# One hybrid encoder layer on one core: the triangular inverse moves from GpSimd and TensorE to VectorE, the weights' low parts from VectorE to GpSimd

## The chip, the core and the metric

The kernel runs on one core of one Trainium2 chip, from one launch. The metric is the device time of one execution in microseconds, lower is better. Engines are named as the profile names them: PE (TensorE matmul) and PEld (its weight loads), DVE (VectorE), ACT (ScalarE), POOL (GpSimd) and SP (SyncE, which here only issues DMAs).

## The reference

One layer for 512 tokens of a new stream and 8 running streams of 16 tokens each, 640 tokens in all, model width 1024, in fp32. Everything is a projection of the same normalised input:

```python
h = rmsnorm(x, norm_g)
proj = h @ w_in                     # 1024 -> 10368 columns
# A: stick-breaking attention, 16 heads of 64 (causal, 128 past keys for the running streams)
# B: RWKV-7 recurrence, 16 heads of 64, one state S (64x64) per head
S = S * w_t + (S @ -kk_t) (kk_t * a_t)^T + v_t k_t^T ;  o_t = S @ r_t
y_a = (o_a * silu(z_a)) @ w_o_a ;  y_b = (norm(o_b) * silu(z_b)) @ w_o_b
x = x + (sigmoid(g_a) * y_a + sigmoid(g_b) * y_b) @ w_out ;  y = rmsnorm(x, final_norm_g)
```

Outputs are y, the new keys and values, the last projected rows of B and the states S.

## The kernel before

**Jobs.** Each projection is cut into jobs of 128 output columns: 81 from `w_in`, 8 each from `w_o_b` and `w_o_a`; `w_out` follows in its own loop. fp32 products are made of three passes of a reduced fp32 type: the weight block `raw` (128 x 1024) is split into a high part `whi` (ACT, `wsplit`, line 486) and a low part `wlo` (DVE, `wlow`, line 494), the input into `xh` and `xl`. A job has two halves of 320 tokens, each 8 blocks of depth by 3 passes, so 48 matmuls (`gemm_range`, line 499). While job i runs, the weights of i+2 are loaded, and i+1 is split: `whi` after the second depth block, `wlo` after the fourth. `raw`, `whi` and `wlo` have two buffers each.

**Streams.** Beside the jobs run generators, called streams: for each of 8 pairs of RWKV heads `prep` (decays, keys, the matrices A of each chunk of 64 tokens), `prep2` (the inverse below), `samp`, `chain` (8 chunk steps one behind the other, each PE, ACT, PE, ACT, PE, DVE), `sstate` and `post`; later for each of 8 pairs of attention heads `aprep` and `attn`. `chain(p)` waits for `chain(p-1)`. A planner (`Clock`, `Driver.run`, line 303) keeps an estimated time for each engine and tile while the program is written out: at each `yield` it lets every stream whose inputs are ready by that estimate issue its next piece, by priority, and then goes on with the job. The result is one fixed order of instructions on each engine; on the chip every engine takes its own in that order, each waiting for its inputs. In the running job there is a `yield` after every second depth block (line 537). `calm()` (line 707) holds a stream back while DVE is planned more than 1.6 us ahead of PE.

**Order of the jobs.** The list `mixed` holds the RWKV projections R, K, V of each pair, `free` those of attention (q, k, v, z) and gates; a mixed job is taken when its condition `soon` holds, otherwise a free one (`job`, line 456). For V of pair p the condition is that `chain(p-3)` is done (line 1519). When `post` of the last pair is done, attention opens (`open_attn`, line 1569), beside the remaining jobs.

**The inverse (`prep2`, line 875).** For each pair and chunk the inverse of (I - A), A strictly lower triangular 64x64, is built. The four diagonal 32x32 blocks of all ten chunks are gathered in `STG` (ACT), transposed by 32x32 on DVE so that each partition holds one block in `INV`, and solved there by forward substitution: step j multiplies row j with column j below it and adds. Before the change this runs on 16x16 blocks, two at a time, on POOL: 14 steps of two instructions for each pair (lines 895 to 901). Then the 16x16 inverses are joined to 32x32 by two rounds of small matmuls (32 and 48 for each pair, lines 916 to 948, with the mask `half`), and after that, unchanged by the diff, to 64x64.

**State of the running streams (`sstate`, line 1094).** For each of two groups the rows X are spread over 4 streams by a mask (`ux`, POOL) and multiplied with the keys: two matmuls of 64 output rows and 256 columns for each group into one PSUM tile, and one addition on DVE.

**Opening (`start`, line 566).** Five token tiles are loaded, squared (ACT), scaled (DVE) and transposed (PE, `put`); `norm_g` is spread over the partitions by a DMA, all loads are issued by SP, and the first sums of squares become factors for tiles 0, 1 and 2, 3 and 4. `warm` are matmuls on zeros that keep PE running.

Of the kernel before, what the change touches and what calls it, by code (L numbers as in the profile page):

```python
# [340 lines left out]
def body(tc, ins, outs, dbg=None):  # L341
# [100 lines left out]
    half = cpool.tile([128, 2], F32, name="half")  # L442
# [51 lines left out]
    def wlow(i):  # L494
        if i < len(jobs):
            j = jobs[i]
            vtt(j.lo, j.raw, j.hi.bitcast(F32), ALU.subtract)

    def gemm_range(i0, i1):
# [6 lines left out]
        for i in range(i0, i1):  # L506
# [9 lines left out]
            for half in range(2):  # L516
# [5 lines left out]
                for k in range(8):  # L522
# [43 lines left out]
    def start():  # L566
        x34 = pers.tile([128, 2, D], F32, tag="H", name="x34")
        srow = pers.tile([88, 3, 128], F32, tag="V", name="srow", bufs=3)
        with pool("start", bufs=1) as sp:
            xt = [sp.tile([128, D], F32, tag="x", name="x", bufs=3) for _ in range(3)]  # L570
            xt += [x34[:, 0], x34[:, 1]]

            def loadx(i):
                dma(out=xt[i], in_=ins["x_prompt"][0, i * 128:(i + 1) * 128, :] if i < 4 else
                    ins["x_sample"].rearrange("b t d -> (b t) d"))
            gb = sp.tile([128, D], F32, name="gb")
            wz = sp.tile([128, 512], BF16, name="wz")
            V.memset(wz, 0.0)
            psw = bank("g")
# [5 lines left out]

            warm(18)
            loadx(0)
            dma(out=gb, in_=ins["norm_g"].partition_broadcast(128).rearrange("p o d -> p (o d)"))
            loadx(1)
            dma(out=ident, in_=ins["consts"][:, 0:128])  # L590
            loadx(2)
            wload(0)
            loadx(3)
            loadx(4)
# [10 lines left out]
            sv = sp.tile([128, 5], F32, name="sv")  # L605
            sr = sp.tile([128, 5], F32, name="sr")
            st = sp.tile([128, 5], F32, name="st")
            junk = sp.tile([128, D], F32, name="junk")
# [4 lines left out]
            def rstd(i0, i1):  # L613
                c = slice(i0, i1)
# [9 lines left out]
            def pscale(i):  # L624
                G.tensor_scalar(out=xt[i], in0=xt[i], scalar1=sr[:, i:i + 1], scalar2=1.0, op0=ALU.mult, op1=ALU.mult)
                gtt(xt[i], xt[i], gb, ALU.mult)

            square(0)
            rstd(0, 1)
            scale(0)  # L630
            square(1)
            square(2)
            rstd(1, 3)
            scale(1)
            put(0, xt[0], "ab")
            warm(6)
            wsplit(0)
            scale(2)
            put(1, xt[1], "ab")
            warm(3)  # L640
            wlow(0)
            square(3)
            square(4)
            put(2, xt[2], "ab")
            warm(0)
# [53 lines left out]
    def setf(*k):  # L699
        flags[k] = True  # L700
# [27 lines left out]
    def prep(p):  # L728
# [9 lines left out]
        if p + 1 < NPAIR:  # L738
            rwkv_load(p + 1)
# [1040 lines left out]
```

## Time and profile before

| what | value |
|---|---|
| three runs, us | 1167.69, 1173.54, 1175.17; median 1173.54 |
| the profiled execution, us | 1171.08 |
| its span from first to last instruction, us | 1169.3 |
| mean granted TensorE clock | 0.99 |

The span is what the profile divides; 1.8 us of the execution lie around it. Busy times are unions of an engine's instructions, those on PE with modelled ends, so a busy PE can still be late. All engines' work is recorded by a helper at line 213, so groups are told apart by tile names; a tile name without a number stands for all its buffers.

### The profile page before, as it was taken

What the parts mean: (1) busy time and instruction counts of PE and PEld (TensorE: products, weight loads), DVE (VectorE), ACT (ScalarE), POOL (GpSimd) and SP (SyncE); (2) the same over time, 40 slices, a digit from 0 to 9 for tenths busy, and PEclk for the clock granted to TensorE, in tenths of its full rate; (3) what the DMA queues carried; (4) which work ended last, traced back from release to release, by engine and by line L of the source; (5) the groups of instructions that cost most, each with busy time, mean ns of one, the idle gap of its engine ahead of it and who ended that gap; (6) DMA issues with size and microseconds to landing.
All of it is one profiled execution on the core that took longest, in us unless ns stands there. A gap on an engine that the chain in (4) does not pass through costs nothing. (4 is left out here: it accounts for less than half of the span.)

```text
span 1169.3 us, 25426 instructions
## 1 busy us (share of the span) xinstructions
PE 1111.5 (95%) x10050; PEld 1037.7 (89%) x10050; DVE 746.2 (64%) x1517; ACT 629.8 (54%) x1347; POOL 390.5 (33%) x605
## 2 busy tenths in 40 slices
PE   6999899989999999999899999999999989999997
PEld 4989899979989989889799899998888878899997
DVE  6485974847765867857767544337777688765424
ACT  5636357646666477466575556445555544522223
POOL 3033315125222243342342513034444454323302
PEclk9999999989999999999999999999999999999999
DMA  5222222213132232133132333369666676366312
GB/s 193 78 89 57 78 66 82 84 50 115 62 95 77 67 93 79 55 88 89 52 93 90 98 103 102 108 184 261 180 161 160 172 216 177 82 197 188 105 56 91
DMA packets 205294, 130.70 MB, mean 112 GB/s; under 512 B 78332, under 2 KB 184696, under 8 KB 205176
## 3 DMA queue, kind: packets, MB, share of 16 engines
q1 hardware_dynamic: 204888, 129.03, 37.8%
q8 instruction: 79, 1.29, 0.4%
q14 instruction: 39, 0.32, 0.1%
q0 software_dynamic: 288, 0.05, 0.0%
HBM read 97.70 MB, written 31.35 MB: 110 GB/s over the span
## 5 line engine op out<-in xcount | busy, mean ns | idle before, releaser
L213 PE MATMUL ps_g<-xh,whi 128*128 128x320 f32 (+1 forms) x1424 | 468.5, 329 | 1.7 <-ACT xh L213 1.3
L213 PE MATMUL ps_g<-xl,whi 128*128 128x320 f32 (+1 forms) x1424 | 443.5, 311 | 3.3 <-DVE xl L213 3.3
L213 PE MATMUL ps_g<-xh,wlo 128*128 128x320 f32 (+1 forms) x1424 | 443.0, 311 | 1.4 <-DVE wlo L213 1.4
L213 PEld LDWEIGHTS ps_g<-xh,whi 128*128 128x128 f32 x1424 | 271.4, 191 | 9.3 <-issue 3.0
L213 PEld LDWEIGHTS ps_g<-xl,whi 128*128 128x128 f32 x1424 | 270.9, 190 | 6.4 <-DVE xl L213 4.5
L213 PEld LDWEIGHTS ps_g<-xh,wlo 128*128 128x128 f32 x1424 | 270.0, 190 | 2.4 <-DVE wlo L213 2.4
L213 DVE TENSOR_TENSOR wlo<-raw,whi 128x1024 fp32r<-128x1024 f32 x97 | 123.6, 1274 | 69.6 <-ACT whi L213 69.0
L213 ACT ACTIVATE whi<-raw 128x1024 fp32r<-128x1024 f32 x97 | 102.7, 1059 | 48.6 <-DMA raw<-in_w_o_a_dram 28.6
L213 DVE TENSOR_TENSOR_SCAN kp<-kp,amsk 128x256 f32<-128x256 f32 (+3 forms) x80 | 73.6, 929 | 27.8 <-ACT kp L213 27.7
L213 POOL TENSOR_TENSOR bt<-bt,amsk 128x128 f32<-128x128 f32 x64 | 44.0, 691 | 124.3 <-ACT bt L213 81.5
L213 POOL TENSOR_TENSOR itmp<-INV 128x28 f32<-128x28 f32 (+6 forms) x112 | 47.0, 420 | 90.8 <-DVE INV L213 82.9
L213 ACT ACTIVATE kp<-ps_a 128x512 f32<-128x512 f32 (+3 forms) x72 | 33.1, 460 | 68.0 <-PE ps_a L213 42.2
L213 ACT ACTIVATE RH<-ps_b 128x128 f32<-128x128 f32 (+1 forms) x64 | 19.4, 302 | 77.8 <-PE ps_b L213 77.4
L213 ACT ACTIVATE sp<-ps_g 128x320 f32<-128x320 f32 x80 | 34.6, 437 | 45.9 <-PE ps_g L213 40.6
L213 ACT ACT_TABLE_LOAD x39 | 50.0, 1283 | 8.9 <-DVE BK L213 5.4
L213 DVE SCALAR_TENSOR_TENSOR X<-ps_b,wc,SW 64x64 f32<-64x64 f32 x96 | 26.7, 278 | 35.7 <-PE ps_b L213 34.9
L213 POOL TENSOR_TENSOR on<-on,V 128x640 f32<-128x640 f32 x8 | 12.4, 1550 | 108.9 <-ACT on L213 108.9
L213 DVE TENSOR_TENSOR bt<-bt,kp 128x511 f32<-128x511 f32 (+4 forms) x72 | 42.4, 588 | 7.7 <-POOL bt L213 0.3
L213 POOL TENSOR_TENSOR INV<-INV,itmp 128x28 f32<-128x28 f32 (+6 forms) x112 | 43.6, 390 | 8.8
L213 PE MATMUL ps_b<-cst,bt 128*128 128x128 f32 x192 | 33.5, 278 | 12.4 <-DVE bt L213 11.8
L213 PE MATMUL ps_g<-olo,mgh 128*128 128x256 f32 x160 | 45.0, 281 | 0.0
L213 PE MATMUL ps_g<-ohi,mgh 128*128 128x256 f32 x160 | 45.0, 281 | 0.0
(252 smaller groups left out, 2319.4 us busy)
## 6 DMA issues: line engine op xcount, KB each, us to landing
raw<-in_w_in_dram SPq DMA_DIRECT2D x81, 512.0 KB
q<-dr_q SPq DMA_DIRECT2D x32, 160.0 KB
Kr<-in_cache_sb_k_dram SPq DMA_DIRECT2D x16, 256.0 KB
Vp<-in_cache_sb_v_dram SPq DMA_DIRECT2D x16, 256.0 KB
raw<-in_w_o_b_dram SPq DMA_DIRECT2D x8, 512.0 KB
raw<-in_w_o_a_dram SPq DMA_DIRECT2D x8, 512.0 KB
oraw<-in_w_out_dram SPq DMA_DIRECT2D x4, 1024.0 KB
dr_zB<-zm SPq DMA_DIRECT2D x8, 320.0 KB
```

What stands on the lines that cost most here:

```text
L213: r = f(*a, **k)
```

## The change

Six things change; nothing else in the program does.

1. `prep2` substitutes on the whole 32x32 blocks, on DVE: 30 steps of two instructions for each pair, step j on (31-j) x j elements, with `calm()` between steps. The two join rounds, `half` and its instructions go.
2. `wlow` runs on POOL, and is written after the second depth block, behind `wsplit`.
3. In the job there is a `yield` after every depth block.
4. `sstate` makes for each group one matmul of 128 output rows and 512 columns, of which half is used, and two additions of 64 rows; it holds no PSUM tile over both groups.
5. The split of w2 and a2 for pair p+1 (`rwkv_split`) is written at the end of the first part of `prep(p)`; V of pair p is called when `post(p-3)` is done.
6. The opening: loads are issued by SP and ACT in turn, `norm_g` arrives as one row and is spread by two matmuls and two ACT copies, one `Sqrt` is issued ahead of the data, each tile has its own factor, and the clearing of `STG` and `ABD` (POOL) comes behind the first `wlo`.

```diff
     def wlow(i):
-            vtt(j.lo, j.raw, j.hi.bitcast(F32), ALU.subtract)
+            gtt(j.lo, j.raw, j.hi.bitcast(F32), ALU.subtract)
...
-                    if (half, k) == ((0, 3) if i else (1, 1)):
+                    if (half, k) == ((0, 1) if i else (1, 1)):
                         wlow(i + 1)
-                    if k % 2:
-                        yield
+                    yield
...
+            ring = (nc.sync.dma_start, nc.scalar.dma_start)
             def loadx(i):
-                dma(out=xt[i], ...
+                ring[i % 2](out=xt[i], ...
...
+            loadx(0)
+            ring[1](out=grow, in_=ins["norm_g"])
+            loadx(1)
+            ring[1](out=ident, in_=ins["consts"][:, 0:128])
+            loadx(2)
+            loadx(3)
+            wload(0)
+            loadx(4)
+            act(out=st, in_=sr, func=AF.Sqrt)
...
+            for hf in range(2):
+                ps = bank("g")
+                c = slice(hf * 512, hf * 512 + 512)
+                mm(ps, lhsT=one, rhs=grow[:, c], start=True, stop=True)
+                act(out=gb[:, c], in_=ps, func=AF.Copy)
...
         act(out=ssft.rearrange("p b j -> p (b j)"), in_=ps[:, 0:264], func=AF.Copy)
+        for t in (STG, *ABD):
+            G.memset(t, 0.0)
...
+    def rwkv_split(p):
+        o = rw[p]
+        wh = o["wh"] = tr.tile([128, 2, 128], F32R, tag="wh", name="wh")
+        wl = o["wl"] = tr.tile([128, 2, 128], F32R, tag="wl", name="wl")
+        act(out=wh, in_=o["wd"], func=AF.Copy)
+        gtt(wl, o["wd"], wh.bitcast(F32), ALU.subtract)
+        if p + 1 < NPAIR:
+            rwkv_load(p + 1)
...
-        tmp = inv.tile([128, 128], F32, tag="Y", name="itmp")
-        for j in range(1, 15):
-            m = 15 - j
-            tv = tmp[:, 0:2 * m * j].rearrange("p (b i s) -> p b i s", b=2, i=m)
-            gtt(tv, DG[:, :, j, 0:j].unsqueeze(2).broadcast_to([128, 2, m, j]),
-                DG[:, :, j + 1:16, j].unsqueeze(3).broadcast_to([128, 2, m, j]), ALU.mult)
-            gtt(DG[:, :, j + 1:16, 0:j], DG[:, :, j + 1:16, 0:j], tv, ALU.add)
-            yield lambda: clk.free["pool"] <= clk.free["pe"] + SLACK
+        tmp = inv.tile([128, 256], F32, tag="Y", name="itmp")
+        eng = V
+        for j in range(1, 31):
+            m = 31 - j
+            tv = tmp[:, 0:m * j].rearrange("p (i s) -> p i s", i=m)
+            eng.tensor_tensor(out=tv, in0=INV[:, j, 0:j].unsqueeze(1).broadcast_to([128, m, j]),
+                              in1=INV[:, j + 1:32, j].unsqueeze(2).broadcast_to([128, m, j]),
+                              op=ALU.mult)
+            eng.tensor_tensor(out=INV[:, j + 1:32, 0:j], in0=INV[:, j + 1:32, 0:j], in1=tv, op=ALU.add)
+            yield calm()
...
-        ps = yield from take("a")
-        pv = ps[:, 0:128].rearrange("p (c s) -> p c s", c=8)
-        for c in range(8):
-            for q in range(4):
-                up = slice(32 * q, 32 * q + 16)
-                i = 32 * (q % 2)
-                mm(pv[32 * q:32 * q + 32, c], lhsT=AB[q][up, c, i:i + 32], rhs=Q[up, 0:16, c],
-                   start=True, stop=True)
...
+            ux = ch.tile([128, 2, 4, 64], F32, tag="ux", name="ux")
...
+            mm(ps, lhsT=BKt[:, 8 + g, :], rhs=ux.rearrange("p h b v -> p (h b v)"), start=True, stop=True)
...
-                g2, s2 = [("post", p - 3)], s2 + [("chain", p - 3)]
+                g2, s2 = [("post", p - 3)], s2 + [("post", p - 3)]
```

Where the instructions now stand, at three places. The first is DVE at the inverse of pair 0 (`INV` holds the blocks, `itmp` the products, `V`, `zm` and `nrm` belong to the job that runs and to `prep`). Before:

```order
L213 STREAM_TRANSPOSE INV<-STG 128x1024
L213 TENSOR_TENSOR wlo<-raw,whi 128x1024
L213 TENSOR_TENSOR V<-ps_a,V 128x320
L213 SCALAR_TENSOR_TENSOR zm<-ps_g,prm,zm 128x319
L213 TENSOR_TENSOR V<-ps_a,V 128x320
L213 TENSOR_SCALAR nrm<-ps_a 128x320
```

and after the change:

```order
L213 TENSOR_TENSOR itmp<-INV 128x168
L213 TENSOR_TENSOR INV<-INV,itmp 128x24x7
L213 TENSOR_SCALAR nrm<-ps_a 128x320
L213 TENSOR_TENSOR itmp<-INV 128x184
L213 TENSOR_TENSOR INV<-INV,itmp 128x23x8
L213 TENSOR_TENSOR itmp<-INV 128x198
L213 TENSOR_TENSOR INV<-INV,itmp 128x22x9
L213 TENSOR_SCALAR nrm<-ps_a 128x320
```

The low parts are gone from DVE, and its other instructions now stand between steps of the substitution, each behind one or more of them.

The second is POOL around `prep` (`wl` is the low part of w2 and a2, `av` and `H` belong to `prep`). Before, the substitution of pair 0 follows the last parts of `prep` of pair 0 and the split for pair 1:

```order
L213 TENSOR_TENSOR H<-R,E_580 64x8x64
L213 TENSOR_TENSOR H<-R,E_580 64x2x64
L213 TENSOR_TENSOR wl<-wd,wh 128x256
L213 TENSOR_TENSOR itmp<-INV 128x28
L213 TENSOR_TENSOR INV<-INV,itmp 128x2x14
```

and after the change, around the same parts of `prep`, here of pair 1:

```order
L213 TENSOR_TENSOR wlo<-raw,whi 128x1024 x2
L213 TENSOR_SCALAR nrm<-av,prm,omka 128x640
L213 TENSOR_TENSOR av<-kkn,av 128x640
L213 TENSOR_TENSOR H<-R,E_1192 64x8x64
L213 TENSOR_TENSOR H<-R,E_1192 64x2x64
L213 TENSOR_TENSOR wlo<-raw,whi 128x1024
L213 TENSOR_TENSOR H<-R,E_1192 64x8x64
L213 TENSOR_TENSOR H<-R,E_1192 64x2x64
L213 TENSOR_TENSOR wlo<-raw,whi 128x1024
```

The small instructions of the substitution have left POOL's queue, and a low part stands in it about once a job, between the parts of `prep`.

The third is PE where the inverse of pair 0 comes back to it. Before, the first join round (32 matmuls on the blocks in `STG` and `AB`) stands between job matmuls:

```order
L213 MATMUL ps_g<-xl,whi 128x322
L213 MATMUL ps_g<-xh,wlo 128x322
L213 MATMUL ps_a<-STG,AB_102 32x16 x32
L213 MATMUL ps_g<-xh,whi 128x322
L213 MATMUL ps_g<-xl,whi 128x322
```

and after the change the first thing that uses the inverse is the step to 64x64, with 16 matmuls:

```order
L213 MATMUL ps_g<-xl,whi 128x322
L213 MATMUL ps_g<-xh,wlo 128x322
L213 MATMUL ps_a<-STG,AB_101 32x32 x16
L213 MATMUL ps_g<-xh,whi 128x322
L213 MATMUL ps_g<-xl,whi 128x322
```

Both join rounds are gone for all 8 pairs. In PE's whole order the runs of job matmuls are broken by other work 310 times before and 356 times after.

## Rows read from the trace of the kernel before

**Rows 1.** Busy us (x instructions) in the RWKV stage and the attention stage

```profile
core 0: us, PE busy (x) PEld busy (x) DVE busy (x) ACT busy (x) POOL busy (x), PEclk, DMA share, GB/s
35.00:715.00 680.00, 654.16 (x6397) 616.40 (x6396) 457.86 (x1027) 407.29 (x862) 220.37 (x399) 0.99 0.27 80
795.00:1031.00 236.00, 220.88 (x1981) 193.76 (x1980) 178.07 (x244) 124.06 (x291) 107.32 (x133) 0.99 0.62 170
```

**Rows 2.** Timeline of PE around both join rounds: start, us, instruction

```profile
130.89 0.31 PE L213 MATMUL ps_g<-xh,wlo 128*128 128x322 f32 x1
131.13 0.74 PE L213 MATMUL ps_a<-STG,AB 16*32 16x16 f32 x64
131.80 0.42 PE L213 MATMUL ps_g<-xh,whi 128*128 128x322 f32 x1
132.06 0.31 PE L213 MATMUL ps_g<-xl,whi 128*128 128x322 f32 x1
...
133.53 0.30 PE L213 MATMUL ps_g<-xh,wlo 128*128 128x322 f32 x1
...
134.77 0.42 PE L213 MATMUL ps_g<-xh,whi 128*128 128x322 f32 x1
```

**Rows 3.** Timeline of PE around one group of sstate

```profile
332.26 0.65 PE L213 MATMUL ps_b<-ux,BKt 128*64 128x256 f32 x4
332.84 0.41 PE L213 MATMUL ps_g<-xh,whi 128*128 128x322 f32 x1
```

**Rows 4.** Timeline of PE around one fp32 product of 320 columns

```profile
105.09 0.70 PE L213 MATMUL ps_a<-kkn,cst 128*128 128x320 f32 x2
...
105.78 0.31 PE L213 MATMUL ps_g<-xl,whi 128*128 128x322 f32 x1
```

**Rows 5.** The two tiles' instructions: count, ns min/median/max

```profile
L213 DVE TENSOR_TENSOR wlo<-raw,whi x97: 1157/1225/2576, 18.7 to 1095.0; 128x1024 fp32r<-128x1024 f32 x97
L213 DVE TENSOR_TENSOR bt<-bt,kp x72: 292/578/1648, 800.0 to 1025.3; 128x511 f32<-128x511 f32 x16, 128x383 f32<-128x383 f32 x16, 128x255 f32<-128x255 f32 x16, 128x127 f32<-128x127 f32 x16
```

**Rows 6.** Timeline of DVE, two instructions of which one needs the other

```profile
7.19 0.16 DVE L213 TENSOR_TENSOR st<-sr 128x1 f32<-128x1 f32 x1
7.39 0.16 DVE L213 TENSOR_TENSOR st<-st,sv 128x1 f32<-128x1 f32 x1
```

**Rows 7.** Busy us by stage, instructions of INV alone: DVE, POOL

```profile
35.00:715.00 680.00, 37.01 (x32) 90.65 (x224) 0.99 0.27 80
```

**Rows 8.** The same of wlo: PE, PEld, DVE

```profile
35.00:715.00 680.00, 302.34 (x972) 184.19 (x971) 76.93 (x61) 0.99 0.27 80
795.00:1031.00 236.00, 73.75 (x238) 44.88 (x239) 20.07 (x15) 0.99 0.62 170
```

**Rows 9.** POOL's two-input instruction on 128 x 640: ns min/median/max

```profile
L213 POOL TENSOR_TENSOR on<-on,V x8: 1536/1545/1568, 231.4 to 767.9; 128x640 f32<-128x640 f32 x8
```

**Rows 10.** Timeline of DVE and POOL, 285 to 288 us

```profile
285.15 1.58 POOL L213 TENSOR_TENSOR av<-kkn,av 128x640 f32<-128x640 f32 x1
...
285.79 2.02 DVE L213 TENSOR_TENSOR wlo<-raw,whi 128x1024 fp32r<-128x1024 f32 x1
286.69 1.26 POOL L213 TENSOR_TENSOR itmp<-INV 128x52 f32<-128x52 f32 x1
```

**Rows 11.** Busy us of DVE in the RWKV stage: instructions of kkn; of sg

```profile
35.00:715.00 680.00, 36.43 (x48) 0.99 0.27 80
35.00:715.00 680.00, 39.32 (x40) 0.99 0.27 80
```

**Rows 12.** Busy us in one stretch of the RWKV stage, columns as in the first group

```profile
450.00:500.00 50.00, 46.17 (x523) 42.39 (x522) 42.04 (x102) 24.85 (x53) 16.02 (x15) 0.97 0.24 73
```

**Rows 13.** Timeline of ACT in the opening

```profile
5.46 1.28 ACT L213 ACT_TABLE_LOAD   x1
```

**Rows 14.** The chain that ended last, near the last weights of w_o_a

```profile
1082.88 1.24 DVE wlo L213
1084.16 5.98 PE ps_g L213 x39
```

More of the change, by code (lines that the diff above doesn't have):

```diff
@@ L622, in scale @@
                 stt(xt[i], xt[i], sr[:, i:i + 1], gb, ALU.mult, ALU.mult)
-            def pscale(i):
-                G.tensor_scalar(out=xt[i], in0=xt[i], scalar1=sr[:, i:i + 1], scalar2=1.0, op0=ALU.mult, op1=ALU.mult)
-                gtt(xt[i], xt[i], gb, ALU.mult)
             square(0)
-            rstd(0, 1)
+            rstd(0)
             scale(0)
             square(1)
-            square(2)
-            rstd(1, 3)
+            rstd(1)
             scale(1)
             put(0, xt[0], "ab")
-            warm(6)
+            warm(4)
+            square(2)
+            rstd(2)
+            scale(2)
             wsplit(0)
-            scale(2)
+            gtt(jobs[0].lo, jobs[0].raw, jobs[0].hi.bitcast(F32), ALU.subtract)
             put(1, xt[1], "ab")
-            warm(3)
-            wlow(0)
+            warm(4)
+            put(2, xt[2], "ab")
+            warm(4)
             square(3)
+            rstd(3)
+            scale(3)
             square(4)
-            put(2, xt[2], "ab")
-            warm(0)
-            rstd(3, 5)
+            rstd(4)
+            scale(4)
             ps = bank("c")
@@ L663, in late @@
         setf("x")
-        vtt(half, cview["msk4"][:, 0:2], cview["msk4"][:, 2:4], ALU.add)
         ps = yield from take("b", srow)
@@ L730, in prep @@
         o = rw[p]
[L731 to L739 removed]
+        if p == 0:
+            yield [o["wd"]]
+            rwkv_split(0)
+        wh, wl = o["wh"], o["wl"]
         sg = tr.tile([128, T], F32, tag="sg", name="sg")
@@ L1097, in sstate @@
         X, BKt, S0T, wc = (o[n] for n in ("X", "BKt", "S0T", "wc"))
-        psn = yield from take("b", X, hold=True)
+        yield [X]
+        sn = ch.tile([128, 8, 64], F32, tag="sn", name="sn")
         for g in range(2):
-            uxs = [ch.tile([128, 4, 64], F32, tag="ux", name="ux", bufs=2) for _ in range(2)]
+            ux = ch.tile([128, 2, 4, 64], F32, tag="ux", name="ux")
             for h in range(2):
-                gtt(uxs[h], X[:, 8 + g, h, :].unsqueeze(1).broadcast_to([128, 4, 64]),
+                gtt(ux[:, h], X[:, 8 + g, h, :].unsqueeze(1).broadcast_to([128, 4, 64]),
                     cview["msk4"].unsqueeze(2).broadcast_to([128, 4, 64]), ALU.mult)
-            yield uxs
+            ps = yield from take("b", ux)
+            mm(ps, lhsT=BKt[:, 8 + g, :], rhs=ux.rearrange("p h b v -> p (h b v)"), start=True, stop=True)
+            pv = ps.rearrange("p (h b v) -> p h b v", h=2, b=4)
+            c = slice(4 * g, 4 * g + 4)
             for h in range(2):
-                mm(psn[RS[h], g * 256:(g + 1) * 256], lhsT=BKt[:, 8 + g, h * 64:(h + 1) * 64],
-                   rhs=uxs[h].rearrange("p b v -> p (b v)"), start=True, stop=True)
-        sn = ch.tile([128, 8, 64], F32, tag="sn", name="sn")
-        vtt(sn, psn.rearrange("p (b v) -> p b v", b=8), S0T, ALU.add)
-        give(psn)
+                vtt(sn[RS[h], c], pv[RS[h], h], S0T[RS[h], c], ALU.add)
+            yield []
         setf("schain", p)
@@ L1739, in body @@
         tr = tr_cm.__enter__()
-        G.memset(STG, 0.0)
-        for t in ABD:
-            G.memset(t, 0.0)
         drv.run(program())
```

81 lines of the change are left out of this document (21 added, 60 removed).

## The prediction

> **What bounds the kernel now.** I read the busy times by stage first. From 35 to 715 us, while the RWKV pairs run beside the jobs, PE is busy 654 of 680 us (96%), DVE 458 (67%), POOL 220 (32%); from 795 to 1031 us, in attention, PE has 221 of 236 us, DVE 178 (75%), POOL 107 (45%) [rows 1]. So PE is the bound, and what the change takes from PE is worth its time as long as nobody makes PE wait more. That last point decides here, since the order on each engine is fixed: a stream's DVE instruction that comes late stops the PE instruction that was written behind it, and every job matmul after that. The second view is therefore a stretch in which DVE was fuller than usual: from 450 to 500 us DVE was busy 84% and PE only 46.2 of 50 us, 92% [rows 12]. The third is the timeline of single instructions, for prices and for what DVE and POOL do to each other.
>
> **PE's own work.** The first join round lies between job matmuls that start at 130.89 and 131.80, and the next one follows after 0.26 us. Job matmuls follow each other at 0.15 us (39 in 5.98 us) [rows 14], so the round costs 0.91 - 0.15 + 0.11 = 0.87 us. The second, from 133.53 to 134.77, costs 1.24 - 0.15 + 0.11 = 1.20 us, taking the same 0.11 behind it [rows 2]. Over 8 pairs that is 16.6 us off PE. A group of `sstate` takes 0.58 us from its start to the next job matmul [rows 3]. A full-height fp32 product of 320 columns takes 105.78 - 105.09 - 0.15 = 0.54 us [rows 4], so one of 512 columns 0.87; against 0.58 + 0.11 that is 0.18 us more, 16 times: +3 us. The order of the changed program breaks the runs of job matmuls 356 times instead of 310, though 16 breaks of the join are gone: 62 new ones. No row prices such a break alone. Below, it is nothing (a stream that is served sooner), above, 0.2 us (the join round's 0.87 less the 0.67 between its start and the next job matmul [rows 2]); I take 0.1, so +6 (0 to +12). In sum PE's work falls by 7.6 us.
>
> **DVE's work.** A two-input fp32 instruction takes 292 ns on 127 elements and 1225 on 1024 [rows 5], so 1.04 ns an element and 0.16 us fixed. Step j of the new substitution has two of (31-j) x j elements; the 60 instructions of a pair have 2 x 4960 = 9920 elements and cost 60 x 0.16 + 9920 x 0.00104 = 19.9 us, 159 us for 8 pairs. Each needs the one before: such a pair of instructions starts 0.20 us apart where one lasts 0.16 [rows 6], which adds 480 x 0.04 = 19 us unless others fill the gaps. The low parts leave: 76.9 us in this stage, 61 of them [rows 8]. The join's five DVE instructions a pair go and two more additions come; by the same 0.16 + 1.04 ns that is 3.6 us less. DVE would have 458 - 77 + 159 + 19 - 4 = 555 of 680 us, 82%, if nobody stood in its way.
>
> **POOL's work.** The old substitution, 90.7 us in 224 instructions, leaves [rows 7]. A two-input instruction on 128 x 640 takes 1.545 us [rows 9], so a low part of 1024 columns about 2.47, twice what DVE needs; 61 of them are 151 us. POOL comes to 220 - 91 + 151 = 280 us, 41%.
>
> **What the two do to each other.** This is the term that decides. At 285.15 POOL begins `av`, which ends at 286.73. DVE begins a low part at 285.79, and that takes 2.02 us instead of 1.22; POOL's next instruction, `itmp`, then lasts 1.26 us and ends just after it [rows 10], where a neighbour of its kind and size needs about 0.3. So a DVE instruction with two inputs in SBUF and a POOL instruction that reads SBUF go one after the other. The Trainium skill says the same and more: by "SBUF — State Buffer", section "Who interferes with whom", a DVE instruction with two SBUF inputs contends with a GpSimd instruction that reads SBUF, and whoever is first keeps the other out for its whole length. The trace agrees with its 0.80 us, and by that rule the exchange of work between the two engines wins no room for either.
>
> Before, the two long kinds (low parts and substitution) met as 1.2 us against 0.4; now the 60 short instructions of each pair stand on DVE, and a low part that slips in between two of them holds the next one up for up to 2.47 us, with everything behind it on DVE: in the order of the changed program these are `nrm`, `zm`, `R`, `K` and, while a chain runs, the chain's `X`, for which PE waits. The price has bounds at 0 (POOL always runs while DVE reads PSUM) and at all of POOL's 280 us. Between them: DVE has a two-input instruction at hand for 178 us of substitution and 36 + 39 us of the others [rows 11], 254 of 680 us, 37%; 37% of 280 is 105 us. DVE then has 660 us to do in 680. It can't be busy 97% where each chain step waits for PE and ACT in turn: the fullest stretch before had 84%, and PE already lost 8% there [rows 12]. At 84% the stage would last 775 us (+95), as the 105 shrink to 97 in a longer stage; at 97%, 680, less the 7.6 us of PE. I take halfway between 84 and 100, 92%: 555 + 100 = 655, divided by 0.92, is 712 us, **+32 us**. The PE sum lies inside it, since PE then waits anyway.
>
> **The rest.** In attention DVE loses 15 low parts, 20.1 us [rows 8], and POOL gains 15 x 2.47 = 37; DVE's scans and products there nearly all have two inputs, so about 60% of the 37 comes back as waiting: 20 against 22, value 0, from -20 to +17. In the last jobs the weights land just in time: the low part took 1.24 us and PE started as it ended [rows 14]; at 2.47 that is +1.2 us (0 to +5, if the other late loads do the same). In the opening a table load of 1.28 us between the first sum and its root [rows 13] moves to where ACT waits for data, and one low part of 1.22 leaves DVE; two ACT copies and one more chain of small DVE steps (some six at 0.2 us [rows 6]) come in: -1 us, from -3 to +2. A rule bears on the loads: by the Trainium skill, "DMA: Bandwidth & Descriptors", section "Issuing engines are not separate DMA queues", a second issuing engine saves only the issue time. No run here shows loads from ACT; by the rule nothing is to be added for them, and I add nothing. Three edits stand at nothing: the clearing on POOL runs while the first jobs do, long before pair 0 writes `ABD`, and costs its length on `wlo` of job 1 if that is late; the earlier split of w2 and a2 lies in the previous pair's chain; the later call of V changes places with free jobs, of which the order still has 17 at the end of the list.
>
> **Sum.** -1 + 32 + 0 + 1.2 = +32 on the profiled execution's 1171.1 us, 1203 us. The median of the runs shown is 2.4 us above that execution, less than a measurement tells; I leave 1203.
>
> **Rivals.**
> *The waits are absorbed.* DVE's idle time in the stage, 125 us by the count without waits, swallows the 105. For it: the substitution has low priority and a chain piece comes in between its steps; against it: at 84% PE already lost 8%. Then PE's 7.6 and the opening's 1 are all: 1171.1 - 8.6 + 1.2 = 1164 us, no change to be told.
> *The waits are absorbed and attention gains.* This one ends on the other side. If in addition half of the 20 us that leave DVE in attention reaches PE, which has 15 us of waiting there, the time is 1154 us, faster. It decides from the point where DVE in that stage falls below about 70% while the RWKV stage stays at 680 us.
> *POOL is late, not DVE.* A low part must be there 42 matmuls after it is written, 42 x 0.15 = 6.3 us, and `whi` comes first. If it stands behind three instructions of `prep` at 1.55 and a second low part, it is ready after 3 x 1.55 + 2 x 2.47 = 9.6 us: PE waits 3.3 us. Twice for each pair is 53 us, 1216 us. For it: POOL's order has `wlo` between the parts of `prep`; against it: jobs with streams beside them last longer than 7 us.
>
> **How the numbers follow.** DVE and POOL in each other's way, with DVE late: 0.50. POOL late: 0.13. Absorbed without gain: 0.17. Absorbed with attention's gain: 0.20. A measurement of this kernel tells about 1%, 12 us, from no change. Slower has the first two, 0.63; within 1% 0.17; faster 0.20. The range goes from 1150 (the faster rival) to 1260 (a stage near the 775 us of 84%); the likeliest case alone has 1180 to 1266.
>
> **What would show it.** Right: the instructions of `INV` on DVE near 20 us a pair unhindered, but some of 2 us and more with a POOL `wlo` over them; DVE at 85 to 95% in the RWKV stage; more PE waiting for DVE's `X`, `AB`, `H` and `STG`, and that stage longer by about 30 us, while PE's instructions of the join are gone. POOL's rival: PE waiting for `wlo` itself. Wrong would be an RWKV stage of 680 us or less, or a substitution whose instructions run unhindered, or ones of 0.1 us each, as then the 159 us are mis-sized.

## The result and the profile after

The changed kernel takes 1275.01 us (median of 4 runs, 1273.96 to 1280.5) against 1174.36 us (4 runs) for the kernel before: a ratio of 1.0875, 95% interval 1.085 to 1.0901. It is slower, as forecast, but by 101 us where 32 were predicted, and outside the range. The time follows from three views.

**Stages.** First both kernels by stage, cut at the same events: the first split of w2 and a2, the first `qh` of attention, attention's last `bt`, the end. Columns are as in [rows 1]: stretch, length, busy time (and instructions) of PE, PEld, DVE, ACT and POOL, granted clock, DMA share, GB/s. Before:

```profile
0.00:38.00 38.00, 28.87 (x158) 22.04 (x159) 21.37 (x46) 21.17 (x37) 10.26 (x16) 0.96 0.50 162
38.00:786.00 748.00, 722.16 (x6870) 682.77 (x6870) 479.69 (x1090) 442.56 (x940) 234.29 (x410) 0.99 0.29 85
786.00:1025.00 239.00, 223.88 (x2003) 197.48 (x2002) 179.52 (x245) 126.03 (x294) 108.12 (x135) 0.99 0.65 176
1025.00:1169.00 144.00, 136.61 (x1025) 135.41 (x1023) 65.66 (x138) 40.02 (x80) 37.87 (x46) 0.99 0.39 129
```

After (the last row is another stretch, used below):

```profile
0.00:47.00 47.00, 37.47 (x159) 27.02 (x161) 24.55 (x57) 21.54 (x41) 15.87 (x18) 0.89 0.36 109
47.00:876.00 829.00, 744.96 (x5658) 700.78 (x5657) 639.10 (x1484) 442.16 (x930) 316.37 (x258) 0.97 0.28 80
876.00:1123.00 247.00, 213.09 (x1920) 186.86 (x1919) 180.44 (x231) 123.82 (x287) 143.04 (x149) 0.97 0.65 163
1123.00:1272.00 149.00, 136.01 (x1009) 133.51 (x1007) 64.11 (x127) 39.31 (x79) 59.20 (x55) 0.99 0.39 125
...
47.00:805.00 758.00, 673.96 (x5164) 630.84 (x5163) 625.20 (x1424) 404.45 (x849) 281.80 (x238) 0.96 0.26 74
```

Length less PE's busy time is PE's waiting: 9.1 + 25.8 + 15.1 + 7.4 = 57 us before, 9.5 + 84.0 + 33.9 + 13.0 = 140 after, 83 more. PE's busy time grows by 20 us, though it has less work. The clock column says why: length times (1 - clock) is 13 us before and 39 after, so the lower clock can have added up to 26 us to PE's busy time (30 by the clocks of the whole span, 0.990 and 0.967). Without these, its busy time would be 6 to 10 us less than before, near the 7.6 that the prediction took off. So: waits +83, clock up to +26, and work, as what remains, about -6.

The stage rows add 9, 81, 8 and 5 us. They hold different numbers of jobs: the RWKV stage has two low parts more than before (72 against 70), attention and the last stage one less each. At 48 x 0.15 = 7.2 us a job, the RWKV stream itself cost 67 us, attention 15 and the last stage 12.

**Who is waited for.** The view of waits of PE (waiting, released by: us, times, longest) for the RWKV stage, before:

```profile
PE ps_b L213 <- POOL sn L213: 8.9, 5, 3.9
PE ps_a L213 <- DVE STG L213: 4.4, 2, 3.0
PE ps_a L213 <- POOL wl L213: 3.3, 3, 2.7
```

and after:

```profile
PE ps_b L213 <- DVE X L213: 24.8, 16, 3.7
PE ps_b L213 <- POOL sn L213: 11.9, 6, 3.5
PE ps_a L213 <- DVE STG L213: 6.4, 3, 2.8
PE ps_a L213 <- DVE BK L213: 5.9, 3, 4.7
PE ps_g L213 <- DVE INV L213: 5.8, 1, 5.8
PE ps_g L213 <- POOL wlo L213: 5.4, 4, 1.9
```

The chain's `X`, which hardly shows before, leads. DVE is late, and POOL's low part itself is a small item. The whole view adds up to 83 us: 62 of them end with DVE, where it was 9 before, and 20 with POOL, where it was 13.

**One such wait.** The timeline of DVE and POOL (start, us, instruction), with the PE rows behind it:

```profile
412.90 0.41 DVE L213 TENSOR_TENSOR itmp<-INV 128x240 f32<-128x240 f32 x1
...
413.28 2.39 POOL L213 TENSOR_TENSOR wlo<-raw,whi 128x1024 fp32r<-128x1024 f32 x1 [1.93 <-issue]
...
413.35 2.58 DVE L213 TENSOR_TENSOR INV<-INV,itmp 128x240 f32<-128x240 f32 x1
415.85 0.81 DVE L213 TENSOR_TENSOR K<-K,nrm 128x640 f32<-128x640 f32 x1
...
417.02 0.41 DVE L213 TENSOR_TENSOR INV<-INV,itmp 128x240 f32<-128x240 f32 x1
...
418.79 0.40 DVE L213 TENSOR_TENSOR INV<-INV,itmp 128x234 f32<-128x234 f32 x1
419.22 0.58 DVE L213 SCALAR_TENSOR_TENSOR X<-ps_b,wc,SW 64x64 f32<-64x64 f32 x2
...
419.95 0.77 PE L213 MATMUL ps_b<-X,H 128*128 128x128 f32 x2 [3.25 <-DVE X L213]
...
421.21 0.47 PE L213 MATMUL ps_g<-xl,whi 128*128 128x322 f32 x1
421.48 0.47 PE L213 MATMUL ps_g<-xh,wlo 128*128 128x322 f32 x1
```

An addition of the substitution that takes 0.41 us alone (the same size at 417.02) takes 2.58, ending just after POOL's low part, which began before it. `K` and six more instructions of the substitution stand behind it, then the chain's `X`, and PE stands for 3.25 us. When it goes on, job matmuls follow each other at 0.27 us instead of 0.15. The stretches show why, with columns as above:

```profile
420.00:424.00 4.00, 4.00 (x19) 4.00 (x20) 3.76 (x14) 1.58 (x6) 0.00 (x0) 0.60 0.03 7
424.00:430.00 6.00, 6.00 (x45) 6.00 (x44) 5.78 (x13) 3.00 (x8) 3.87 (x3) 1.00 0.13 33
```

The granted clock is 0.60 right after the wait, mostly the 1.2 GHz level, and then 1.00, the 2.4 GHz level, again: the wait is paid a second time.

**The priced instructions.** Groups of the substitution on DVE and of POOL's low part after (count, busy us, mean ns, idle before), answering to [rows 5, 7, 8]:

```profile
L213 DVE TENSOR_TENSOR itmp<-INV 128x30 f32<-128x30 f32 (+14 forms) x240 | 113.3, 472 | 6.4
L213 DVE TENSOR_TENSOR INV<-INV,itmp 128x30 f32<-128x30 f32 (+14 forms) x240 | 111.5, 464 | 8.2
L213 POOL TENSOR_TENSOR wlo<-raw,whi 128x1024 fp32r<-128x1024 f32 x97 | 237.6, 2450 | 427.0 <-ACT whi L213 373.6
```

The low part takes 2.45 us, predicted 2.47. The substitution takes 225 us in sum where 159 were predicted for it unhindered. The view of the tile has its shortest, median and longest instruction in ns:

```profile
L213 DVE TENSOR_TENSOR itmp<-INV x240: 172/352/3491, 118.0 to 775.1; 128x30 f32<-128x30 f32 x8, 128x84 f32<-128x84 f32 x8, 128x130 f32<-128x130 f32 x8, 128x168 f32<-128x168 f32 x8
```

The median, 0.35 us, is near the price of 159 us / 480 = 0.33; the longest, 3.49 us, is ten times that.

**The opening.** DVE and POOL at the third scaling, and where the first factors for the projections are made, then PE:

```profile
17.14 3.46 DVE L213 SCALAR_TENSOR_TENSOR x<-x,sr,gb 128x1024 f32<-128x1024 f32 x1
...
17.17 2.34 POOL L213 TENSOR_TENSOR wlo<-raw,whi 128x1024 fp32r<-128x1024 f32 x1 [9.47 <-ACT whi L213]
...
28.52 3.33 POOL L213 TENSOR_TENSOR wlo<-raw,whi 128x1024 fp32r<-128x1024 f32 x1 [3.78 <-ACT whi L213]
...
29.56 2.33 DVE L213 TENSOR_SCALAR omu<-prm 128x33 f32<-128x33 f32 x1
...
34.03 0.64 PE L213 MATMUL ps_g<-xh,whi 128*128 128x322 f32 x1 [3.18 <-ACT xh L213]
```

Both low parts collide. The scaling takes 3.46 us instead of 1.28 (its row starts 0.03 us ahead of the low part's and yet it is the one that waits, so at this distance the start times don't tell who was first), and `omu`, 33 elements, takes 2.33; behind `omu` stand ACT's `latm` and `xh`, for which PE waits 3.18 us.

### The profile page after: what moved, and what is told of

Read it like the earlier page. It is cut to its first block, busy times and chain, and to the rows that moved or that the text cites. A ratio compares the mean times of both kernels' runs of the same rounds, so it can differ in the third digit from the quotient of the medians.

```text
span 1272.2 us, 23081 instructions
## 1 busy us (share of the span) xinstructions
PE 1131.5 (89%) x8740; PEld 1048.2 (82%) x8741; DVE 908.2 (71%) x1897; ACT 626.8 (49%) x1335; POOL 534.5 (42%) x478
## 5 line engine op out<-in xcount | busy, mean ns | idle before, releaser
L213 PE MATMUL ps_g<-xh,whi 128*128 128x320 f32 (+1 forms) x1424 | 480.2, 337 | 20.6 <-DVE INV L213 5.8
L213 PE MATMUL ps_g<-xh,wlo 128*128 128x320 f32 (+1 forms) x1424 | 449.2, 315 | 5.4 <-POOL wlo L213 5.4
L213 POOL TENSOR_TENSOR wlo<-raw,whi 128x1024 fp32r<-128x1024 f32 x97 | 237.6, 2450 | 427.0 <-ACT whi L213 373.6
L213 PEld LDWEIGHTS ps_g<-xl,whi 128*128 128x128 f32 x1424 | 276.5, 194 | 12.2 <-DVE xl L213 9.4
L213 DVE TENSOR_TENSOR itmp<-INV 128x30 f32<-128x30 f32 (+14 forms) x240 | 113.3, 472 | 6.4
L213 DVE TENSOR_TENSOR INV<-INV,itmp 128x30 f32<-128x30 f32 (+14 forms) x240 | 111.5, 464 | 8.2
L213 DVE TENSOR_TENSOR bt<-bt,kp 128x511 f32<-128x511 f32 (+4 forms) x72 | 58.2, 809 | 9.8 <-POOL bt L213 3.2
L213 PE MATMUL ps_b<-cst,bt 128*128 128x128 f32 x192 | 34.2, 281 | 25.2 <-DVE bt L213 23.5
L213 PE MATMUL ps_b<-X,H 128*128 128x128 f32 x160 | 32.0, 299 | 24.7 <-DVE X L213 24.6
L213 PEld LDWEIGHTS ps_b<-X,H 128*128 128x128 f32 x160 | 24.7, 195 | 31.7 <-issue 18.2
L213 PEld LDWEIGHTS ps_b<-cst,bt 128*128 128x128 f32 x192 | 23.1, 142 | 30.7 <-issue 24.3
```

The lines of the kernel that those rows point to most:

```text
L213: r = f(*a, **k)
```

## The experiments

The theory, *sharing*: a two-input instruction of DVE and one of POOL that reads SBUF go one after the other, DVE is then too full, and PE waits. Its rivals: POOL is late by itself; the substitution costs by its own time or length; the small edits do it; the order is at fault. Each run below states its ratio to the kernel before, measured beside it, with the 95% interval.

### One part alone

`e3_inv_alone`: part 1 of the change on the kernel before.

> The kernel before with the substitution on 32x32 blocks on VectorE alone (join gone); low parts stay on VectorE, order of V, yields, state and opening as before. By the change with the low parts put back (1258 us) VectorE should again have some 650 us of its own and 50 of waiting in the RWKV stage: if an overfull VectorE is the cause, 1235 to 1250 us. If the cause is one of the small edits (yields, state of the running streams, V's call), this one is at 1160 to 1180, since PE is rid of the join.

`e4_low_alone`: part 2 on the kernel before.

> The kernel before with the low parts on GpSimd alone, written after the second depth block. GpSimd then has the old substitution and the low parts, about 360 us of its own in the RWKV stage, and VectorE some 410: if GpSimd that comes late to PE (the products sn and ux, the low part itself) is the cause of what the run with the inverse put back still lost, 1220 to 1240 us. If the small edits are, 1175 or less.

`e7_three_small`: parts 3, 4 and 5. `e5_open_alone`: part 6. `e6_open_low`: part 6 with one line as before:

```diff
-            gtt(jobs[0].lo, jobs[0].raw, jobs[0].hi.bitcast(F32), ALU.subtract)
+            wlow(0)                       # vtt, on VectorE
```

> The kernel before with the three small edits alone: a yield after every depth block, the state of the running streams by matmuls of full height, and the earlier split with V's later call. By the prediction +3 for the state and +6 for the breaks: 1176 to 1185 us. If they carry the loss, 1220 or more; if the finer yields serve the streams better, 1165 or less.

> The kernel before with the rebuilt opening alone (job 0's low part on GpSimd with it). If the 10 us lost at the start of the changed kernel are the opening's own (the factor of norm_g comes by way of matmuls and two copies, so the first scaling starts at 10.7 instead of 8.0 us, and the third collides with GpSimd's low part), this takes 1178 to 1183 us. If they come from the low parts of jobs 1 and 2 on GpSimd behind the clearing, the opening alone gives 1170 to 1174, as first predicted.

> The kernel before with the rebuilt opening, but job 0's low part on VectorE as before. If the loss of the opening is the collision of the third scaling (3.46 us instead of 1.28) with GpSimd's low part, 1172 to 1175 us; if it is the chain by way of the matmuls and copies of norm_g, as slow as the opening alone, 1178.

| run | us, median | ratio |
|---|---|---|
| inverse alone | 1268.71 | 1.0817 (1.0779 to 1.0856) |
| low parts alone | 1221.66 | 1.0415 (1.0378 to 1.0452) |
| three small edits | 1179.29 | 1.0058 (1.004 to 1.0075) |
| opening alone | 1178.4 | 1.0041 (1.0021 to 1.0062) |
| opening, low part on VectorE | 1177.26 | 1.004 (1.0017 to 1.0064) |

The inverse alone costs 96 us, nearly the whole loss, and more than its 1235 to 1250. The low parts alone cost 48. The small edits are the 6 us expected, the opening 4 to 6. That the opening's loss is the collision with job 0's low part fell: on VectorE it costs the same within the interval. The singles add up to some 155 us, the whole to 101. That they don't add is no surprise: each large part alone leaves one engine with both works (DVE with the low parts, POOL with the old substitution), and the other part takes one of them off it.

### One part taken back

`e1_low_back`: the changed kernel, low parts on DVE at (0,3), as the lines below show. `e2_inv_back`: the changed kernel without part 1.

```diff
-            gtt(j.lo, j.raw, j.hi.bitcast(F32), ALU.subtract)
+            vtt(j.lo, j.raw, j.hi.bitcast(F32), ALU.subtract)
...
-                    if (half, k) == ((0, 1) if i else (1, 1)):
+                    if (half, k) == ((0, 3) if i else (1, 1)):
```

> The changed kernel with every low part back on VectorE, at its old place; the rest as changed. The changed kernel lost about 10 us in the opening, 64 beside the RWKV pairs, 21 in attention and 8 at the end. If the two engines go one after the other at SBUF (sharing), VectorE gets 77 us of its own work back in the RWKV stage and loses about as much waiting, since GpSimd then reads SBUF for some 100 us instead of 240: that stage stays within 20 us, attention and the end come back, about 1235 us. If GpSimd's low parts are simply late (late GpSimd), that stage falls by 40 us and more: about 1185. If the substitution's own time on VectorE is the whole cost and nothing collides, the 77 us come on top: 1270 or more.

> The changed kernel with the inverse of before (16x16 blocks on GpSimd, joined by matmuls); low parts stay on GpSimd, the rest as changed. Sharing: VectorE is rid of the substitution's 225 us, the RWKV stage comes back to some 690 us, while opening, attention and end stay as changed: about 1215. Late GpSimd: GpSimd has 91 us more to do in front of the low parts, so the kernel gets slower than the changed one, 1290. Own time of the substitution: as with sharing, about 1210; this run does not tell these two apart.

Measured: 1258.01 us, ratio 1.073 (1.0701 to 1.0758), and 1252.24, ratio 1.0686 (1.0657 to 1.0714). Taking back either half of the exchange gives back only 17 and 23 of 101 us. The RWKV stage of the first, and of the second:

```profile
42.00:879.00 837.00, 765.09 (x5758) 715.83 (x5757) 653.55 (x1559) 449.38 (x940) 140.99 (x186) 0.96 0.28 82
```

```profile
44.00:838.00 794.00, 727.83 (x6802) 690.69 (x6801) 437.56 (x1046) 442.95 (x937) 386.13 (x480) 0.96 0.27 81
```

The greatest waits of PE in the second:

```profile
PE ps_b L213 <- POOL sn L213: 31.0, 6, 8.5
PE ps_a L213 <- DVE STG L213: 10.0, 3, 4.9
```

In the first, as sharing said, DVE is just as full with the low parts of its own (654 us of 837) as with POOL in its way (639 of 829); but the time, 1258 us, is 23 above the 1235 of sharing and lies between it and the 1270 of a substitution that costs by its own time. Where its loss sits is shown by the table in the section on the prediction. The Trainium skill, "Perfetto Trace Analysis", section "Optimizing Scalar/DVE Operations", warns that moving work between GpSimd and VectorE might not help, as they share a read port; 1258 against 1275 us agrees. In the second, both prices were wrong, the 1215 of sharing and the 1290 of a late POOL: DVE has room (438 of 794), but POOL now has 386 us of work with `sn` behind it, and PE waits 31 us for `sn`, up to 8.5 at a time. This is the rival of the late POOL; it is large in this kernel and small in the changed one (11.9 us for `sn`, 8.9 before).

### Reading or being busy

`e8_low_copy`: the changed kernel, low parts replaced by ACT's copies. `e9_no_read`: POOL as busy, but writing only.

```diff
-            gtt(j.lo, j.raw, j.hi.bitcast(F32), ALU.subtract)
+            G.memset(j.lo.bitcast(F32), 0.0)
+            G.memset(j.lo[:, 0:5].bitcast(F32), 0.0)
+            nc.gpsimd.memset(j.lo[:, 0:6].bitcast(F32), 0.0)
+            gtt(j.lo[:, 0, 0:8], j.raw[:, 0, 0:8], j.hi[:, 0, 0:8].bitcast(F32), ALU.subtract)
```

> The changed kernel with the low parts left out: from job 1 on ScalarE copies the raw weights in their place, so neither VectorE nor GpSimd has them (the products are then of other numbers). Sharing: the substitution's instructions fall from 225 us in sum to under 175, and the RWKV stage by 40 us or more, attention by 15: about 1205 us. Own time of the substitution without collisions: the instructions keep their 225 us and the RWKV stage stays, about 1250. ScalarE gets 1.05 us a job more, which both take as free.

> The changed kernel with the low parts left out, but GpSimd kept as busy: instead of the subtraction it clears the same tile in three pieces, some 2.4 us that read nothing, and subtracts 8 columns, so that it still waits for the high part (the products are then of other numbers). Sharing (a GpSimd instruction that reads SBUF keeps VectorE's two-input ones out): the substitution's instructions fall from 225 to under 180 us and the time to 1185 to 1205, as with the low parts copied by ScalarE (1189). Late GpSimd (it is only the queue in front of sn, ux and the low part itself): 1250 to 1275, as GpSimd is as full as before.

Measured: 1189.22 us, ratio 1.0138 (1.0116 to 1.016), and 1204.99, ratio 1.027 (1.0239 to 1.0301). The RWKV stage of the copies:

```profile
42.00:811.00 769.00, 744.96 (x5792) 707.37 (x5792) 555.98 (x1484) 513.62 (x1014) 136.16 (x186) 0.99 0.30 89
```

and that of the clearing:

```profile
44.00:820.00 776.00, 738.32 (x5724) 700.19 (x5723) 565.91 (x1484) 446.16 (x938) 327.24 (x478) 0.98 0.30 88
```

The substitution's groups in the clearing run:

```profile
L213 DVE TENSOR_TENSOR INV<-INV,itmp 128x30 f32<-128x30 f32 (+14 forms) x240 | 91.0, 379 | 8.3
L213 DVE TENSOR_TENSOR itmp<-INV 128x30 f32<-128x30 f32 (+14 forms) x240 | 87.2, 364 | 6.2
```

The clearing against the changed kernel is the clearest pair. POOL is busy 327 us here and 316 there, DVE has the same 1484 instructions, yet needs 566 us instead of 639; the substitution falls from 225 to 178 us, and the kernel by 70 us. So POOL's reading is what costs, not its being busy: sharing is shown, and taking the low parts' reading away is worth 73 us of DVE and 70 of the 101 us. The planner's order isn't the same in the two kernels, so the 70 can hold some effect of order; but the instructions of the substitution show the cause directly, the longest takes 1.67 us instead of 3.49. The Trainium skill, "SBUF — State Buffer", section "Who interferes with whom", says that a GpSimd instruction that only writes doesn't contend with a two-input one of VectorE; these 566 against 639 us agree.

### Room or length of the substitution

With few collisions (its substitution takes 174 us), the inverse alone still costs 96 us. `g1_inv_alone_copy`: that kernel without low parts on DVE; `g2_before_copy`: the same for the kernel before.

```diff
-            vtt(j.lo, j.raw, j.hi.bitcast(F32), ALU.subtract)
+            act(out=j.lo, in_=j.raw, func=AF.Copy)
```

> The kernel before with the substitution on VectorE, and the low parts left out (ScalarE copies the raw weights in their place; the products are of other numbers). If VectorE's room is the cause, its work in the RWKV stage falls from 684 to some 600 us and the time from 1269 to 1170 to 1195. If each pair's wait for a substitution of 20 us and more is, it stays above 1230.

> The kernel before with the low parts left out in the same way. If the time follows VectorE's room only where that is short, this gains little, 1155 to 1170 us, with VectorE at some 440 us in the RWKV stage; if every microsecond on VectorE counts, 1120 or less.

Measured: 1211.63 us, ratio 1.0318 (1.0288 to 1.0348), and 1169.12, ratio 0.9966 (0.9949 to 0.9982). The first lies between both expectations: room gives back 57 of the 96 us. The low parts on DVE cost the kernel before only 5 us, where DVE has room: without them it is 55% busy in the RWKV stage, with them 64%. Here the RWKV stage of the inverse alone, then that of the same without low parts, with its last stage:

```profile
38.00:871.00 833.00, 770.04 (x5795) 721.21 (x5794) 639.82 (x1535) 446.88 (x938) 146.28 (x187) 0.94 0.28 82
```

```profile
40.00:825.00 785.00, 749.92 (x5821) 712.52 (x5820) 548.46 (x1461) 515.12 (x1013) 137.35 (x187) 0.97 0.30 87
...
1073.00:1213.00 140.00, 122.72 (x878) 118.97 (x878) 52.14 (x121) 43.67 (x84) 38.97 (x46) 0.91 0.39 130
```

What is left is partly at the end: here attention ends so late against the jobs that only 7 low parts (those of w_o_a) come after it, where the kernel before has 10. PE waits for the last outputs of attention (`oAh`, `oAl`), stands 17.3 of 140 us, and the stage's clock is 0.91. By stages at 7.2 us a job, the profiled execution loses 18 us there, 16 in attention and 8 in the RWKV stage; so a longer wait of each pair for its inverse accounts for little more than those 8. Why attention is longer isn't separated by these runs.

### Order

The planner that sets the order knows the collisions or doesn't. `e10_port_after`, `e11_port_before`: changed kernel and kernel before with

```diff
+        if port:
+            for a, b in self.port["pool" if eng == "dve" else "dve"]:
+                if a <= st < b:
+                    st = b
+            self.port[eng] = self.port[eng][-60:] + [(st, st + dur)]
         self.free[eng] = st + dur
...
-            self.clk.note(e, d, [_name(x) for x in ins], [_name(out)], lat)
+            ps = any(_name(x).startswith("ps_") for x in aps)
+            two = op in ("tensor_tensor", "scalar_tensor_tensor", "tensor_tensor_scan") and not ps
+            self.clk.note(e, d, [_name(x) for x in ins], [_name(out)], lat,
+                          port=two if e == "dve" else e == "pool" and op != "memset")
```

`e12_port_yield`, `f2_port_yield_split`, `f4_port_yield_state_split`: the kernel before with that planner and part 3; parts 3 and 5; parts 3, 4 and 5. `f1_yield_alone`: the kernel before with part 3. `f3_no_yield`: the changed kernel without part 3 (`if k % 2:` ahead of the `yield` again).

> The changed kernel, whose planner now knows that a two-input instruction of VectorE and one of GpSimd that reads go one after the other; so the order changes and nothing else. If the cost of the collisions is one of order (streams' instructions are written behind work that the chip does later than planned), PE's waits fall and the time goes to 1220 to 1245. If it is one of room (VectorE has 680 us to do in that stage in any order), it stays at 1260 to 1280.

> The kernel before with the same knowledge in its planner, nothing else. Its VectorE waits for 32 us in the RWKV stage and 24 in attention. If order matters, 1160 to 1170 us; if it doesn't, 1170 to 1180; if the planner then holds streams back for collisions that do not come, 1185 and more.

> The kernel before with that planner and the yield after every depth block. The prediction priced the 62 breaks of the finer yields at 0.1 us each: 6 us above the run with the planner alone. If a stream that is served sooner is worth more than the break, it lies below that run.

> The kernel before with the yield after every depth block, nothing else. By the prediction's price of a break (0.1 us, 0 to 0.2) it is 3 to 9 us slower, 1176 to 1183. If finer yields save time whatever the planner knows, 1150 to 1165. If they pay only where the planner holds streams back, 1170 to 1176.

> The changed kernel with the yield only after every second depth block, as before. If the finer yields cost their breaks, 1265 to 1272 us, a little faster than the changed kernel; if they save time there too, 1285 to 1310.

> The kernel before with the planner that knows of the collisions, the finer yields, and the earlier split of w2 and a2 with V's later call. If the earlier split takes its GpSimd and ScalarE steps off the start of a pair, 1155 to 1162; if V's later call only moves jobs, 1160 to 1168, as without it.

> As the run with planner, yields, split and V's call, and the state of the running streams by matmuls of full height as well: by the prediction's term +3 us against it; if the PSUM tile that is no longer held over both groups counts for more, 3 us and more below it.

| run | us, median | ratio |
|---|---|---|
| changed, planner | 1309.7 | 1.1142 (1.1093 to 1.1191) |
| before, planner | 1201.57 | 1.0231 (1.0206 to 1.0257) |
| before, planner, yields | 1163.52 | 0.9914 (0.9886 to 0.9943) |
| before, yields | 1169.03 | 0.9966 (0.9952 to 0.9979) |
| changed, no yields | 1293.24 | 1.1018 (1.0989 to 1.1047) |
| before, planner, yields, split | 1169.06 | 0.9965 (0.9947 to 0.9982) |
| the same and the state | 1166.14 | 0.9945 (0.9924 to 0.9965) |

The planner alone makes both kernels worse: the kernel before to the time of the third case (that streams held back are the reason isn't read from a trace), the changed one beyond both of its cases, and its substitution still takes 234 us. So this knowledge doesn't mend the changed kernel; that another order would isn't excluded. The finer yields, priced as a loss, save 3 to 4 us alone, 18 in the changed kernel and 38 beside the planner. With the planner they give the fastest kernel of the study, 10 us below the kernel before; the split and V's later call take some 6 of these back, beyond both of that run's cases, and the state gives 2 to 3 again. The gain of planner and yields lies in attention:

```profile
769.00:1008.00 239.00, 233.41 (x2081) 208.48 (x2080) 186.59 (x245) 130.17 (x302) 107.70 (x135) 0.99 0.65 182
```

The stage is as long as before and holds 17 low parts instead of 15; PE waits 6 us in it, where the kernel before has 15.

## Why the prediction was right and wrong

**Right: the direction, the mechanism, most prices.** A POOL low part was to take 2.47 us (2.45), the substitution to meet POOL's low part in instructions of 2 us and more (2.58, 3.49), PE to wait for `X`, and the cost to come from collisions (the clearing run: 70 us). PE's work was to fall by 7.6 us; the rows leave 6 to 10. The sum of DVE's work held, from the high side: 555 + 100 = 655 us were predicted for the stretch of [rows 1], and the corresponding stretch after, 47 to 805 (both end 71 us before attention), has 625. The 105 us of waiting were 73 for the low parts in the whole RWKV stage, above which the substitution lost some 15 us more to other POOL instructions (175 with the copies, 159 predicted).

**Wrong: "I take halfway between 84 and 100, 92%".** This divisor is the step that failed. With less work than predicted, the stretch took 758 us instead of 712: DVE was 82% busy in it, not 92. The other end, the 84% of [rows 12], gave 775 us and +95, and stood in the text as a bound. (Its 97 us should be 92, by the same share of 254 in 775 us, which gives 770.) A share that was reached once, at a loss, was taken as the floor of what the engine does, where it was about the ceiling of a whole stage. By the count of jobs the RWKV stream cost 67 us instead of 32, half of what the forecast was short; the other half are the terms further below.

The runs put numbers to it. The table has the RWKV stage up to the end of the last substitution, and the rest of the stage behind it, where the last chains run:

| kernel | length, us | DVE busy share | PE waits, us | PE waits behind it, us | clock behind it |
|---|---|---|---|---|---|
| before, low parts copied | 602 | 61% | 17 | 0 | 1.00 |
| before | 639 | 68% | 26 | 0 | 1.00 |
| before, planner, yields | 628 | 69% | 25 | 2 | 1.00 |
| inverse alone, low parts copied | 683 | 76% | 26 | 9 | 0.93 |
| changed, low parts copied | 671 | 79% | 22 | 2 | 0.98 |
| changed, POOL clearing | 673 | 80% | 36 | 1 | 1.00 |
| inverse alone | 748 | 82% | 35 | 28 | 0.63 |
| changed, planner | 770 | 82% | 50 | 30 | 0.73 |
| changed, low parts on DVE | 753 | 83% | 48 | 24 | 0.74 |
| changed, no yields | 733 | 83% | 74 | 2 | 1.00 |
| changed | 728 | 84% | 84 | 0 | 1.00 |

With the substitution on DVE this stretch comes out at 76 to 84%, in no kernel above, and roughly the more DVE has to do, the longer it is. That is a mean, and no limit of the engine. Single stretches go higher, and what PE loses in them differs; here 50 us of the changed kernel, then of the inverse alone:

```profile
397.00:447.00 50.00, 42.34 (x303) 39.85 (x301) 47.67 (x121) 25.19 (x59) 18.80 (x15) 0.97 0.26 76
```

```profile
538.00:588.00 50.00, 48.58 (x394) 45.23 (x394) 47.41 (x108) 28.62 (x54) 7.14 (x13) 1.00 0.27 82
```

DVE is 95% busy in both, and PE waits 7.7 us in the one and 1.4 in the other. So the share alone doesn't tell what PE pays. In the changed kernel, with POOL's low parts in DVE's way, PE waits inside the stretch. With the low parts on DVE it waits less there, and a good part of the loss comes behind it. The rest of the stage of the changed kernel, then of the inverse alone:

```profile
775.00:876.00 101.00, 100.91 (x764) 99.19 (x763) 29.42 (x113) 56.39 (x125) 42.77 (x25) 1.00 0.42 123
```

```profile
786.00:871.00 85.00, 56.56 (x299) 46.19 (x299) 26.94 (x107) 37.07 (x92) 14.46 (x14) 0.63 0.22 59
```

DVE is about 30% busy in both, but in the second PE has 1.1 job matmuls a us beside the chains instead of 5.5, waits 28 us and runs at a clock of 0.63. It had run more jobs before (3416 job matmuls against 2854); that it ran short of them for this reason fits, but no run tests it. The two kernels with both works on POOL are left out: there PE waits 66 us (inverse put back) and 34 (low parts alone) at a DVE share of 59% and 63%, so DVE isn't the only engine that can make it wait.

**Missing: the clock.** Each longer wait was priced once. The profile of before had the second price in it: in [rows 12] the clock stands at 0.97 where PE waited for 3.8 of 50 us. After, it's up to 26 to 30 us of the 101.

**Mis-sized: opening, attention, last jobs, yields.** The opening's -1 was +4 to 6 alone and +9 in the whole kernel. Most of the 4.2 us that the first job starts later (24.03 instead of 19.81 us) come with the collision of the third scaling: with the low part on VectorE it starts at 20.37. But without it the kernel ends no earlier; the rest are `omu` behind the low part and the clock behind it, 0.89 in that stage. Attention's 0 was +15, inside its bounds of -20 to +17: PE waits 34 instead of 15 us there, 23.5 of them for DVE's `bt`. The last jobs' +1.2 were +12, above the bound of +5; 5.5 of them are waits for POOL's low part. The yields' +6 were -3 to -4 alone: only the break was priced, not the stream that comes sooner.

**The rivals.** Absorbed waits, with or without attention's gain, fell. The late POOL has 10.8 us of waits for the low part in the changed kernel, not 53; it came where POOL kept both works (31 us for `sn`). A case that was not on the list comes as near in time: DVE too full with few collisions, as in the inverse alone (1269 us), where DVE keeps its low parts and much of the loss comes behind the last substitution.

## What to carry to other kernels

Where several streams share a fixed order, ask not whether an engine has idle time left but what share of a whole stage it was ever busy; a short stretch doesn't tell that. Here it was 76 to 84% in every kernel with the substitution on VectorE. The share goes with the stage's length and doesn't tell the waits: look also at the end of the stage, where the streams may outlast the work that fills the bound engine. Work moved between VectorE and GpSimd wins no room where both read SBUF at the same time; what reads PSUM on VectorE, or only writes on GpSimd, went unhindered here. Price a wait of TensorE twice, once for its length and once for the work behind it at the lower clock.

## What the runs showed of the hardware that was not expected

- **A GpSimd instruction that only writes leaves VectorE's two-input instructions alone.** With 327 us of POOL, more than half of it clearing, the substitution took 178 us; with 316 us, nearly all reading, 225.
- **Some one-input instructions wait too.** `omu`, a TENSOR_SCALAR of 33 elements, lasted from 29.56 to the end of POOL's low part, 2.33 us, where its neighbour `omka` takes 0.16. In the RWKV stage two TENSOR_SCALARs on `Oa` that began under a low part took 2.28 and 2.39 us, with a median of 0.31 for the others, while a RECIPROCAL of `nrm` there took 1.10 and 1.15 against 1.14.
- **What reads PSUM on VectorE isn't held.** The chain's `X`, with one input in PSUM, took 0.29 us (median) in the 17 cases where it began under a low part of the changed kernel, and 0.28 in the other 79.
- **The clock falls behind a wait of PE.** After the wait of 3.25 us that ended at 419.95 it stood at 0.60 from 420 to 424; over the whole span it is 0.967 where the kernel before has 0.990.
